# A mixture-of-experts stage: the float32 tile at place 1, gating in three steps 1024 wide, transposes evicted three tiles later

## The chip, the cores and the metric

One core of a Trainium2 chip runs the whole program. The time is that of the device for one execution, in microseconds (us), as the median of several runs; a profile is one more execution with its own time.

## The reference

Three transformer blocks follow each other on 256 tokens of width 1024. The change touches only the last part of the third, a mixture of 32 experts with 4 chosen for each token:

```python
N_EXPERTS = 32; TOP_K = 4; D_FF_EXPERT = 1024
SWIGLU_ALPHA = 1.702; SWIGLU_LIMIT = 7.0

def clamped_swiglu(u):
    u_glu, u_lin = u[..., ::2], u[..., 1::2]
    u_glu = jnp.minimum(u_glu, SWIGLU_LIMIT)
    u_lin = jnp.clip(u_lin, -SWIGLU_LIMIT, SWIGLU_LIMIT)
    return u_glu * jax.nn.sigmoid(SWIGLU_ALPHA * u_glu) * (u_lin + 1.0)

def moe_ffn(h, router_w, router_b, w1, b1, w2, b2):
    ...
    gate = jax.nn.softmax(top_val, axis=-1)
    ...
    def block_ffn(args):
        xb, e = args
        act = clamped_swiglu(xb @ w1[e] + b1[e])
        return act @ w2[e] + b2[e]
    ...
    return jnp.zeros((T, D), h.dtype).at[sorted_tok].add(contrib)
```

## The kernel before

In the mixture the experts are sorted by their number of tokens and taken one a round, `r` = 0 to 31. A round streams twelve weight tiles of 128x2048 float32 (1 MB each) from memory: eight for the first product (`up`, here u0 to u7) and four for the second (`down`, here d0 to d3). `down` in round `r` belongs to an expert of an earlier round, `r - 2` from round 6 on.

**Where a tile lives.** The SP queue issues every load in program order. Five buffers (`raw`) and a sixth (`rawm`) are used in turn, so the load of a tile waits until the tile six places ahead of it has been released.

**What is done with a tile.** Most tiles are split (`split`, L509 and L510): ACT writes a rounded copy `whi`, then DVE subtracts it and writes the rest `wlo`. TensorE multiplies the gathered tokens with both. Three pairs of `whi`, `wlo` exist; a pair comes free when TensorE has done with its `wlo`. A split tile releases its `raw` buffer when DVE has read it. To unload ACT and DVE, two tiles of a round are not split (`parts` returns `True`): TensorE reads them as plain float32 from `raw`, in eight matmuls, and releases the buffer itself. One is in `up`, one is d1 in `down`. This holds for rounds 4 to 31 ("small" experts, up to 64 tokens); rounds 0 to 3 ("big", up to 128 tokens, `r < BIGS`) have no plain tile and three matmul terms for each tile.

**Gating.** Two small experts share one tile `ml` of 128 partitions, 64 each. `take` brings the product of a round from PSUM into `ml`: ACT copies the gate and up values across the partitions (L1894), DVE adds the other half (L1895). In each even round from 6 to 30 the pair before is gated (`activate`): a minimum (L1874) and a two-sided bound (L1876) on DVE, Silu on ACT (L1875), and the product on DVE (L1880). TensorE then transposes the result (`turn`, tile `atp`, L1911), and ACT and DVE evict it into the split pair `tp` (L1921, L1922), which `down` reads. `weigh` (L1937, L1938) evicts the product of `down` as `yh`, `yl`; `combine` (L1948) multiplies it back to the tokens, and DVE adds that to `acc` (L1956).

**What sets the order.** The order on TensorE, ACT and DVE is that of the code. `at(r, slot, f)` puts a step at a slot of a round: slots 0 to 7 are the tiles of `up`, 8 to 11 those of `down`. In slot k the split of tile k comes first, then its `whi` matmuls, then the steps of the slot, then its `wlo` matmuls. `pair_of(step, r, slot)` runs `step` at `slot` and what it returns (the eviction) two slots later.

An even round with `activate` is called an even stage below, the round after it an odd one; together they stream 24 tiles.

Of the kernel before, what the change touches and what calls it, by code (L numbers as in the profile page):

```python
# [13 lines left out]
F32R = mybir.dt.float32r  # L14
# [10 lines left out]
ALPHA = 1.702  # L25
# [409 lines left out]
class Net:  # L435
# [1202 lines left out]
    def moe(s, x, nm, ctx):  # L1638
# [163 lines left out]
        def parts(what, r, k):  # L1802
# [4 lines left out]
            if not big(r) and k == (3 if what == "up" else 1):  # L1807
                return True, (w,)
# [69 lines left out]
        def gated(b, n):  # L1878
            ns, us = slice(n * 512, n * 512 + 512), slice(1024 + n * 512, 1536 + n * 512)
            nc.vector.scalar_tensor_tensor(b[:, us], b[:, us], 1.0, b[:, ns], op0=ALU.add, op1=ALU.mult)  # L1880

        def take(r, n):

            p = P[r]
            if n == 0 and (big(r) or r % 2 == 0):
                A[r] = mp.tile([128, 2048], F32, name="ml", tag="ml", bufs=1)
            if big(r):
                gate_(A[r], p[:, 0:1024], p[:, 1024:2048], n)
                return
            b = A[r - r % 2]  # L1890
            own = slice(64 * (r % 2), 64 * (r % 2) + 64)
            other = slice(64 - 64 * (r % 2), 128 - 64 * (r % 2))
            ns = slice(n * 1024, n * 1024 + 1024)
            nc.scalar.activation(b[own, ns], p[other, ns], AF.Copy)  # L1894
            nc.vector.tensor_add(b[own, ns], b[own, ns], p[own, ns])  # L1895

        def activate(r, n):
            b = A[r]
            if not big(r):
                gate_(b, b[:, 0:1024], b[:, 1024:2048], n)  # L1900
            gated(b, n)

        def turn(r, n):

            b = A[r]
            if n == 0:
                P["t"] = s.bank("atp", (128, 8, 128), "p2", 1), mp.tile([128, 8, 2, 128], F32R, name="tp",
                                                                       tag="tp", bufs=1)
            p, t = P["t"]
            for k in range(4 * n, 4 * n + 4):  # L1910
                nc.tensor.transpose(p[:, k], b[:, 1024 + k * 128:1152 + k * 128], ident)  # L1911
            if big(r):
                hi, lo = t[:, :, 0], t[:, :, 1]
# [337 lines left out]
```

## Time and profile before

| | |
|---|---|
| median of 3 runs | 2924.27 us (2922.13 to 2938.32) |
| profiled execution | 2929.59 us, of which the span from first to last instruction is 2927.8 us |
| mean granted TensorE clock | 0.968 of full speed |
| busy shares of the span | TensorE matmul 95%, DVE 77%, ACT 58% |
| bytes moved by DMA | 727.41 MB, mean 248 GB/s |

A busy share is over the whole program. The mixture is the last third, from about 1690 us on.

### The profile page before, as it was taken

How to read it: one execution, taken by the hardware profiler on the slowest of the kernel's cores; microseconds unless marked ns; L12 is line 12 of the kernel's file. 1: busy time of each engine (PE TensorE's matmuls, PEld its weight loads, DVE VectorE, ACT ScalarE, POOL GpSimd, SP SyncE). 2: the span in 40 equal slices, each digit the busy share in tenths (PEclk: the TensorE clock that was granted, in tenths of full speed). 3: DMA queues.
4: the chain of work that ended last, by engine and by line, in shares of the span. 5: the costliest groups of instructions: out<-in, count | busy, mean ns of one | idle time of the engine just before them, and what ended most of it. 6: DMA issues, size and time to landing. Idle time of an engine off the chain costs nothing. (4 is left out here: it accounts for less than half of the span.)

```text
span 2927.8 us, 46001 instructions
## 1 busy us (share of the span) xinstructions
PE 2778.3 (95%) x17764; PEld 2391.2 (82%) x17764; DVE 2256.4 (77%) x3587; ACT 1691.8 (58%) x2676; POOL 3.3 (0%) x10
## 2 busy tenths in 40 slices
PE   9999999999999999999999989989998999999986
PEld 9999999999989999899998677766666666666664
DVE  7676787787777778887777558788888888888885
ACT  6554454644545447644665456666666666666663
POOL 0000000000000000000000000000000000000000
PEclk9999999999999999999999989999999999999998
DMA  7655566576536664366423238788888888888884
GB/s 281 230 203 185 182 243 251 189 272 239 194 116 223 252 238 159 116 244 245 144 101 110 92 149 315 291 324 345 348 354 346 347 355 347 349 343 347 350 356 162
DMA packets 102146, 727.41 MB, mean 248 GB/s; under 512 B 11352, under 2 KB 12888, under 8 KB 14368
## 3 DMA queue, kind: packets, MB, share of 16 engines
q1 hardware_dynamic: 99648, 719.64, 64.6%
q10 hardware_dynamic: 2272, 4.75, 0.5%
q8 instruction: 143, 2.34, 0.3%
q14 instruction: 83, 0.68, 0.1%
HBM read 723.28 MB, written 1.06 MB: 247 GB/s over the span
## 5 line engine op out<-in xcount | busy, mean ns | idle before, releaser
L510 DVE TENSOR_TENSOR wlo<-raw,whi 128x512 fp32r<-128x512 f32 (+1 forms) x1267 | 1247.1, 1019 | 217.7 <-ACT whi L509 212.5
L509 ACT ACTIVATE whi<-raw 128x512 fp32r<-128x512 f32 (+1 forms) x1267 | 1065.1, 891 | 516.1 <-issue 280.1
L515 PE MATMUL gu<-xh,whi 128*128 128x256 f32 (+1 forms) x1760 | 499.7, 284 | 1.7 <-ACT whi L509 1.7
L517 PE MATMUL gu<-xh,wlo 128*128 128x256 f32 (+1 forms) x1760 | 497.5, 283 | 0.7 <-DVE wlo L510 0.7
L516 PE MATMUL gu<-xl,whi 128*128 128x256 f32 (+1 forms) x1760 | 498.0, 283 | 0.0
L1843 PE MATMUL p<-whi,gx 128*128 128x512 f32 x1040 | 300.9, 417 | 49.1 <-ACT whi L509 49.1
L517 PEld LDWEIGHTS gu<-xh,wlo 128*128 128x128 f32 x1760 | 333.8, 190 | 1.1 <-DVE wlo L510 0.9
L515 PEld LDWEIGHTS gu<-xh,whi 128*128 128x128 f32 x1760 | 332.4, 189 | 2.5 <-ACT whi L509 2.1
L516 PEld LDWEIGHTS gu<-xl,whi 128*128 128x128 f32 x1760 | 332.9, 189 | 0.3
L1843 PE MATMUL p<-wlo,gx 128*128 128x512 f32 x912 | 283.1, 435 | 40.4 <-DVE wlo L510 39.5
L1843 PEld LDWEIGHTS p<-whi,gx 128*128 128x128 f32 x1040 | 199.0, 196 | 108.7 <-ACT whi L509 64.6
L1843 PEld LDWEIGHTS p<-wlo,gx 128*128 128x128 f32 x912 | 170.7, 204 | 103.4 <-DVE wlo L510 75.7
L517 PE MATMUL acc<-fh,wlo 128*128 128x256 f32 x880 | 245.5, 280 | 0.0
L516 PE MATMUL acc<-fl,whi 128*128 128x256 f32 x880 | 244.9, 280 | 0.1
L515 PE MATMUL acc<-fh,whi 128*128 128x256 f32 x880 | 242.4, 280 | 0.0
L510 DVE TENSOR_TENSOR wlo<-rawm,whi 128x2048 fp32r<-128x2048 f32 x63 | 144.0, 2286 | 51.0 <-ACT whi L509 51.0
L516 PEld LDWEIGHTS acc<-fl,whi 128*128 128x128 f32 x880 | 165.8, 188 | 0.6 <-DVE fl L510 0.4
L517 PEld LDWEIGHTS acc<-fh,wlo 128*128 128x128 f32 x880 | 165.2, 188 | 0.0
L515 PEld LDWEIGHTS acc<-fh,whi 128*128 128x128 f32 x880 | 163.2, 187 | 1.2 <-ACT fh L509 0.8
L1865 PE MATMUL p<-whi,tp 128*128 128x512 f32 x464 | 152.2, 418 | 1.8 <-ACT whi L509 1.8
L1865 PE MATMUL p<-wlo,tp 128*128 128x512 f32 x400 | 128.7, 403 | 16.9 <-DVE wlo L510 16.9
L509 ACT ACTIVATE whi<-rawm 128x2048 fp32r<-128x2048 f32 x63 | 120.4, 1912 | 27.8 <-DMA rawm<-wmoe 26.4
(704 smaller groups left out, 4918.2 us busy)
## 6 DMA issues: line engine op xcount, KB each, us to landing
raw<-wmoe SPq DMA_DIRECT2D x321, 1024.0 KB, 7.4
raw<-wf SPq DMA_DIRECT2D x164, 1024.0 KB, 4.9
rawm<-wmoe SPq DMA_DIRECT2D x63, 1024.0 KB, 6.7
raw<-win SPq DMA_DIRECT2D x26, 1024.0 KB, 4.8
raw<-wada SPq DMA_DIRECT2D x24, 1024.0 KB, 4.8
raw<-wmod SPq DMA_DIRECT2D x24, 1024.0 KB, 4.9
raw<-wain SPq DMA_DIRECT2D x14, 1024.0 KB, 4.8
raw<-wkvf SPq DMA_DIRECT2D x9, 1024.0 KB, 4.8
```

Of the source, the lines that this page charges most:

```text
L509: a = s.nc.scalar.activation(hi, x, AF.Copy)
L510: s.nc.vector.tensor_sub(lo, x, hi.bitcast(F32))
L515: mm(out, w[0], x[0], start=first, stop=False, skip_group_check=True)
L516: mm(out, w[0], x[1], start=False, stop=False, skip_group_check=True)
L517: mm(out, w[1], x[0], start=False, stop=last, skip_group_check=True)
L1843: mm(p[:, ns], xi, wi[:, ns], start=k == 0 and j == 0, stop=False, skip_group_check=True)
L1865: mm(p[:, n * 512:n * 512 + 512], xi, wi[:, c:c + 512], start=k == 0 and j == 0, stop=k == 7 and j == len(ts) - 1, skip_group_check=True)
```

## The change

The plain tile of `up` is u1 instead of u3. `activate` becomes three steps in three slots: both bounds on DVE at slot 0 (`bound`), Silu on ACT at slot 1 (`silu`), the product on DVE at slot 2 (`gated`), each over 1024 columns in one instruction where there were two of 512. All eight transposes are issued at slot 3 (half of them stood at slot 4), and their two evictions at slots 6 and 7 instead of 5 and 6. The two ACT copies of `take` stand together at slot 10, ahead of both additions (`fold`). For the big rounds `take` only bounds, and Silu moves into the next round's slot 1. The tail after the last round is written with the new steps.

```diff
-            if not big(r) and k == (3 if what == "up" else 1):
+            if not big(r) and k == 1:
                 return True, (w,)
...
-        def gate_(b, g, u, n):
-            ns, us = slice(n * 512, n * 512 + 512), slice(1024 + n * 512, 1536 + n * 512)
-            nc.vector.tensor_scalar(b[:, ns], g[:, ns], 7.0, None, op0=ALU.min)
-            nc.scalar.activation(b[:, ns], b[:, ns], AF.Silu, scale=ALPHA)
-            nc.vector.tensor_scalar(b[:, us], u[:, ns], 7.0, -7.0, op0=ALU.min, op1=ALU.max)
...
+        def bound(b, g, u):
+            nc.vector.tensor_scalar(b[:, 0:1024], g, 7.0, None, op0=ALU.min)
+            nc.vector.tensor_scalar(b[:, 1024:2048], u, 7.0, -7.0, op0=ALU.min, op1=ALU.max)
+
+        def silu(r):
+            nc.scalar.activation(A[r][:, 0:1024], A[r][:, 0:1024], AF.Silu, scale=ALPHA)
+
+        def gated(r):
+            b = A[r]
+            nc.vector.scalar_tensor_tensor(b[:, 1024:2048], b[:, 1024:2048], 1.0, b[:, 0:1024], op0=ALU.add,
+                                           op1=ALU.mult)
...
+            own, other = halves(r)
+            for ns in (slice(0, 1024), slice(1024, 2048)):
+                nc.scalar.activation(A[r - r % 2][own, ns], p[other, ns], AF.Copy)
...
-            for k in range(4 * n, 4 * n + 4):
+            for k in range(8):
                 nc.tensor.transpose(p[:, k], b[:, 1024 + k * 128:1152 + k * 128], ident)
...
             if t >= 0:
-                for n in range(2):
-                    at(r, n, lambda t=t, n=n: activate(t, n))
-                    pair_of(lambda t=t, n=n: turn(t, n), r, 3 + n)
+                at(r, 0, lambda t=t: activate(t))
+                at(r, 1, lambda t=t: silu(t))
+                at(r, 2, lambda t=t: gated(t))
+
+                def turned(t=t, r=r):
+                    out = turn(t)
+                    at(r, 6, lambda: out(0))
+                    at(r, 7, lambda: out(1))
+                at(r, 3, turned)
             if r != 0:
-                at(r, 9 if r == BIGS else 10, lambda r=r: take(r, 0))
-                at(r, 9 if r == BIGS else 11, lambda r=r: take(r, 1))
+                at(r, 9 if r == BIGS else 10, lambda r=r: take(r))
+                at(r, 9 if r == BIGS else 10, lambda r=r: fold(r, 0))
+                at(r, 9 if r == BIGS else 11, lambda r=r: fold(r, 1))
```

ACT, from d2 of an odd round into the even round 20 behind it. Before (`whi<-raw` and `whi<-rawm` are splits, `ml<-p` a copy of `take`, `ml<-ml` a Silu, `yh` a `weigh`, `tp` an eviction of transposes):

```order
L509 ACTIVATE whi<-rawm 128x2048
L1894 ACTIVATE ml<-p_25096 64x1024
L509 ACTIVATE whi<-raw 128x2048
L1894 ACTIVATE ml<-p_25096 64x1024
L509 ACTIVATE whi<-raw 128x2048
L1875 ACTIVATE ml<-ml 128x512
L509 ACTIVATE whi<-raw 128x2048
L1937 ACTIVATE yh<-p_25285,gs 128x512
L1875 ACTIVATE ml<-ml 128x512
L509 ACTIVATE whi<-raw 128x2048
L1937 ACTIVATE yh<-p_25285,gs 128x512
```

The same place after the change:

```order
L509 ACTIVATE whi<-rawm 128x2048
L1893 ACTIVATE ml<-p_25052 64x1024 x2
L509 ACTIVATE whi<-raw 128x2048 x2
L1940 ACTIVATE yh<-p_25241,gs 128x512
L1877 ACTIVATE ml<-ml 128x1024
L509 ACTIVATE whi<-raw 128x2048
L1940 ACTIVATE yh<-p_25241,gs 128x512
L509 ACTIVATE whi<-raw 128x2048
L509 ACTIVATE whi<-rawm 128x2048
L509 ACTIVATE whi<-raw 128x2048 x2
L1929 ACTIVATE tp<-atp 128x8x64
```

Both copies now precede the split of d3, one Silu of twice the width stands ahead of the split of u2, and four splits (u3 to u6) stand between the last `yh` and the first eviction; before, two (u4 and u5) did.

DVE in the same even round, from the split of u0 (`wlo`) on. Before:

```order
L510 TENSOR_TENSOR wlo<-raw,whi 128x2048
L1874 TENSOR_SCALAR ml<-ml 128x512
L1876 TENSOR_SCALAR ml<-ml 128x512
L1880 SCALAR_TENSOR_TENSOR ml<-ml 128x512
L510 TENSOR_TENSOR wlo<-raw,whi 128x2048
L1938 SCALAR_TENSOR_TENSOR yl<-p_25285,gs,yh 128x512
L1874 TENSOR_SCALAR ml<-ml 128x512
L1876 TENSOR_SCALAR ml<-ml 128x512
L1880 SCALAR_TENSOR_TENSOR ml<-ml 128x512
L510 TENSOR_TENSOR wlo<-raw,whi 128x2048
```

After:

```order
L510 TENSOR_TENSOR wlo<-raw,whi 128x2048
L1873 TENSOR_SCALAR ml<-ml 128x1024
L1874 TENSOR_SCALAR ml<-ml 128x1024
L1941 SCALAR_TENSOR_TENSOR yl<-p_25241,gs,yh 128x512
L510 TENSOR_TENSOR wlo<-raw,whi 128x2048
L1941 SCALAR_TENSOR_TENSOR yl<-p_25241,gs,yh 128x512
L1881 SCALAR_TENSOR_TENSOR ml<-ml 128x1024
L510 TENSOR_TENSOR wlo<-raw,whi 128x2048
L510 TENSOR_TENSOR wlo<-rawm,whi 128x2048
L510 TENSOR_TENSOR wlo<-raw,whi 128x2048
```

The bounds follow the split of u0 in both, but the product now stands behind the split of u2, and no split of u1 is left between them.

TensorE at the start of `up` in the same even round (`p<-raw` is the plain tile, eight matmuls that are printed as x4 by their operands; `atp` the transposes). Before:

```order
L1843 MATMUL p_25342<-whi,gx 128x512 x4
L1843 MATMUL p_25342<-wlo,gx 128x512 x4
L1843 MATMUL p_25342<-raw,gx 128x512 x4
L1911 MATMUL atp<-const,ml 128x128 x4
L1843 MATMUL p_25342<-whi,gx 128x512 x4
```

After:

```order
L1843 MATMUL p_25298<-wlo,gx 128x512 x4
L1843 MATMUL p_25298<-raw,gx 128x512 x4
L1843 MATMUL p_25298<-whi,gx 128x512 x4
L1843 MATMUL p_25298<-wlo,gx 128x512 x4
L1843 MATMUL p_25298<-whi,gx 128x512 x4
L1918 MATMUL atp<-const,ml 128x128 x8
L1843 MATMUL p_25298<-wlo,gx 128x512 x4
```

The plain tile, which stood right ahead of the transposes, now stands behind the first split tile, and the transposes stand inside the fourth tile.

## Rows read from the trace of the kernel before

**Rows 1.** The page's second part: GB/s in the 40 equal slices of the span (73.2 us each).

```profile
GB/s 281 230 203 185 182 243 251 189 272 239 194 116 223 252 238 159 116 244 245 144 101 110 92 149 315 291 324 345 348 354 346 347 355 347 349 343 347 350 356 162
```

**Rows 2.** Windows: the stretch; its length; busy time of PE, PEld, DVE, ACT and POOL with instructions; granted clock; DMA share; GB/s. The second row holds the rounds from the first even stage to the last, the others pieces of one pair of rounds.

```profile
2476.00:2514.00 38.00, 32.50 (x120) 21.54 (x118) 32.38 (x20) 25.07 (x17) 0.00 (x0) 1.00 1.01 423
...
1930.00:2870.00 940.00, 852.43 (x3404) 598.60 (x3404) 775.34 (x596) 626.59 (x536) 0.00 (x0) 0.93 0.87 347
...
2442.50:2453.00 10.50, 8.53 (x16) 4.90 (x17) 8.99 (x9) 6.61 (x5) 0.00 (x0) 0.51 0.81 321
```

**Rows 3.** Timeline of ACT: start, duration, line, operation, [idle before, and what ended it]. The first Silu of the even stages of rounds 8 and 30.

```profile
2003.10 0.63 ACT L1875 ACTIVATE ml<-ml 128x512 f32<-128x512 f32 x1 [3.28 <-DVE ml L1874]
...
2799.77 0.63 ACT L1875 ACTIVATE ml<-ml 128x512 f32<-128x512 f32 x1 [3.28 <-DVE ml L1874]
```

**Rows 4.** What waited for what from 1930 to 2870 us: total us, times, longest. (SPq is the queue that issues the loads.)

```profile
DVE wlo L510 <- ACT whi L509: 87.3, 93, 4.6
...
ACT tp L1921 <- PE atp L1911: 98.9, 13, 8.4
ACT ml L1875 <- DVE ml L1874: 82.7, 27, 3.3
...
SPq L490 <- PE p L1865: 133.2, 26, 5.6
SPq L490 <- PE p L1843: 132.9, 26, 6.9
```

**Rows 5.** Timeline of ACT in one pair of rounds, from d2 of the odd round ahead (2426.13) to the next such d2 (2497.65).

```profile
2426.13 1.92 ACT L509 ACTIVATE whi<-rawm 128x2048 fp32r<-128x2048 f32 x1 [0.65 <-DMA rawm<-wmoe]
2428.07 1.02 ACT L1894 ACTIVATE ml<-p 64x1024 f32<-64x1024 f32 x1
...
2437.90 0.63 ACT L1875 ACTIVATE ml<-ml 128x512 f32<-128x512 f32 x1 [3.28 <-DVE ml L1874]
...
2458.00 0.60 ACT L1921 ACTIVATE tp<-atp 128x512 fp32r<-128x512 f32 x1 [7.59 <-PE atp L1911]
...
2482.73 1.91 ACT L509 ACTIVATE whi<-rawm 128x2048 fp32r<-128x2048 f32 x1 [0.76 <-DMA rawm<-wmoe]
2485.22 1.92 ACT L509 ACTIVATE whi<-raw 128x2048 fp32r<-128x2048 f32 x1 [0.58 <-DMA raw<-wmoe]
...
2497.65 1.91 ACT L509 ACTIVATE whi<-rawm 128x2048 fp32r<-128x2048 f32 x1 [3.06 <-DMA rawm<-wmoe]
```

**Rows 6.** Timeline of DVE in the same even stage.

```profile
2430.40 1.22 DVE L1895 TENSOR_TENSOR ml<-ml,p 64x1024 f32<-64x1024 f32 x1
...
2437.44 0.42 DVE L1874 TENSOR_SCALAR ml<-ml 128x512 f32<-128x512 f32 x1
2437.78 0.42 DVE L1876 TENSOR_SCALAR ml<-ml 128x512 f32<-128x512 f32 x1
2438.56 0.69 DVE L1880 SCALAR_TENSOR_TENSOR ml<-ml 128x512 f32<-128x512 f32 x1 [0.36 <-ACT ml L1875]
2440.36 2.29 DVE L510 TENSOR_TENSOR wlo<-raw,whi 128x2048 fp32r<-128x2048 f32 x1 [1.10 <-ACT whi L509]
2442.69 0.75 DVE L1938 SCALAR_TENSOR_TENSOR yl<-p,gs,yh 128x512 fp32r<-128x512 f32 x1
...
2458.63 0.69 DVE L1922 SCALAR_TENSOR_TENSOR tp<-atp,tp 128x512 fp32r<-128x512 f32 x1 [5.01 <-ACT tp L1921]
...
2463.84 2.28 DVE L510 TENSOR_TENSOR wlo<-raw,whi 128x2048 fp32r<-128x2048 f32 x1
2466.05 0.68 DVE L1956 TENSOR_TENSOR acc<-acc,cbp 128x512 f32<-128x512 f32 x1
2466.65 2.28 DVE L510 TENSOR_TENSOR wlo<-raw,whi 128x2048 fp32r<-128x2048 f32 x1
```

**Rows 7.** Timeline of TensorE in the same even stage: the split tiles u0 to u2, the plain u3, the second group of transposes and what follows it, the `whi` terms of two successive tiles with a combine between them (2458.74, 2461.53), and d0 and the plain d1.

```profile
2435.79 1.08 PE L1843 MATMUL p<-whi,gx 128*128 128x512 f32 x4
2437.58 1.20 PE L1843 MATMUL p<-wlo,gx 128*128 128x512 f32 x4 [0.71 <-DVE wlo L510]
2440.38 1.20 PE L1843 MATMUL p<-whi,gx 128*128 128x512 f32 x4 [1.60 <-ACT whi L509]
2442.71 2.07 PE L1843 MATMUL p<-wlo,gx 128*128 128x512 f32 x4 [1.13 <-DVE wlo L510]
2446.29 2.07 PE L1843 MATMUL p<-whi,gx 128*128 128x512 f32 x4 [1.51 <-ACT whi L509]
...
2450.49 4.73 PE L1843 MATMUL p<-raw,gx 128*128 128x512 f32 x8
...
2457.37 0.60 PE L1911 MATMUL atp<-const,ml 128*128 128x128 f32 x4
...
2458.74 1.07 PE L1843 MATMUL p<-whi,gx 128*128 128x512 f32 x4
...
2461.53 1.08 PE L1843 MATMUL p<-whi,gx 128*128 128x512 f32 x4
...
2468.98 0.74 PE L1865 MATMUL p<-wlo,tp 128*128 128x512 f32 x2 [0.20 <-DVE wlo L510]
...
2470.48 3.60 PE L1865 MATMUL p<-raw,tp 128*128 128x512 f32 x8
2473.52 1.03 PE L1865 MATMUL p<-whi,tp 128*128 128x512 f32 x2
```

More of the change, by code (lines that the diff above doesn't have):

```diff
@@ L1884, in take @@
+        def take(r):
             p = P[r]
-            if n == 0 and (big(r) or r % 2 == 0):
+            if big(r) or r % 2 == 0:
                 A[r] = mp.tile([128, 2048], F32, name="ml", tag="ml", bufs=1)
             if big(r):
-                gate_(A[r], p[:, 0:1024], p[:, 1024:2048], n)
+                return bound(A[r], p[:, 0:1024], p[:, 1024:2048])
+            own, other = halves(r)
+            for ns in (slice(0, 1024), slice(1024, 2048)):
+                nc.scalar.activation(A[r - r % 2][own, ns], p[other, ns], AF.Copy)
@@ L1889, in take, with halves, fold @@
+        def halves(r):
+            h = 64 * (r % 2)
+            return slice(h, h + 64), slice(64 - h, 128 - h)
+        def fold(r, n):
+            if big(r):
                 return
-            b = A[r - r % 2]
-            own = slice(64 * (r % 2), 64 * (r % 2) + 64)
-            other = slice(64 - 64 * (r % 2), 128 - 64 * (r % 2))
+            own, _ = halves(r)
             ns = slice(n * 1024, n * 1024 + 1024)
-            nc.scalar.activation(b[own, ns], p[other, ns], AF.Copy)
-            nc.vector.tensor_add(b[own, ns], b[own, ns], p[own, ns])
@@ L1897, in activate @@
-        def activate(r, n):
-            b = A[r]
[L1899 to L1909, printed above, removed]
-            for k in range(4 * n, 4 * n + 4):
+            b = A[r - r % 2][own, ns]
@@ L1911, in turn, with activate @@
+            nc.vector.tensor_add(b, b, P[r][own, ns])
+        def activate(r):
+            if not big(r):
+                bound(A[r], A[r][:, 0:1024], A[r][:, 1024:2048])
+        def turn(r):
+            b = A[r]
+            p = s.bank("atp", (128, 8, 128), "p2", 1)
+            t = mp.tile([128, 8, 2, 128], F32R, name="tp", tag="tp", bufs=1)
+            for k in range(8):
                 nc.tensor.transpose(p[:, k], b[:, 1024 + k * 128:1152 + k * 128], ident)
             if big(r):
-                hi, lo = t[:, :, 0], t[:, :, 1]
+                hi, lo = A[r] = t[:, :, 0], t[:, :, 1]
@@ L2024, in moe @@
                         bias2(c2)
-                    take(0, 0)
-                    take(0, 1)
+                    take(0)
                     for k in range(8, 12):
@@ L2044, in moe @@
                     run(r, 11)
-            for n in range(2):
-                activate(30, n)
+            activate(30)
+            silu(30)
             weigh(29, 0)
             weigh(29, 1)
-            outs = [turn(30, n) for n in range(2)]
+            gated(30)
+            out = turn(30)
             for c2 in range(4):
@@ L2052, in moe @@
                 if c2 % 2:
-                    outs[c2 // 2]()
+                    out(c2 // 2)
             for _ in down(30, 32):
```

12 lines of the change are left out of this document (2 added, 10 removed).

## The prediction

> **What bounds the kernel now.** I first looked at the bytes by slices, because the mixture streams its weights: the last sixteen slices sit between 315 and 356 GB/s with little variation, which looks like a limit [rows 1]. It is not one. Cut finer, the mean of 347 GB/s over the rounds with even stages hides 38 us at 423 GB/s, with the DMA engines busy all the time, and poorer stretches between [rows 2]. In the good stretch tiles land 2.49 us apart (2482.73 and 2485.22, both splits having waited for the transfer) [rows 5]. A pair of rounds streams 24 tiles, so it needs 24 x 2.49 = 59.8 us. It takes more: from the first Silu of round 8 to that of round 30 there are eleven pairs in 796.7 us, 72.4 us each [rows 3]. The pair shown, from one d2 to the next, takes 2497.65 - 2426.13 = 71.5 us [rows 5], 11.7 above its transfers. The mixture is held up by something that recurs in every pair.
>
> The list of waits names it: ACT waits for the transposes 13 times, 98.9 us in all, and for DVE's bound before a Silu, 82.7 us; the load queue waits for TensorE, which alone releases plain tiles, 266 us [rows 4]. The three timelines of one even stage show the order of events. Gating alternates between DVE and ACT twice, and each time a split of ACT is queued behind a Silu: DVE stands idle 0.36 us, then 1.10 [rows 6], and again so in the second half. TensorE starves in these gaps (0.71, 1.60, 1.13 and 1.51 us) [rows 7], and the granted clock over the next 10.5 us is 0.51, the lower of its two levels, 1.2 GHz [rows 2]. There it comes to the plain u3, which takes 2450.49 to about 2455.05, and only behind that do the transposes stand; the second group ends at 2457.97 [rows 7]. ACT's eviction was queued ahead of the split of u6, so ACT idles 7.59 us [rows 5] and DVE 5.01 [rows 6]. Meanwhile every buffer is full, and the transfers stop. So what decides is the chain of DVE and ACT through an even stage, and then the plain d1, whose release lets the queue go on.
>
> **The change, by replaying this stage with the new order.** I keep the start (d2 on ACT at 2426.13) and use the durations of these rows.
>
> *Take.* Both copies precede the split of d3 on ACT: 2428.07 + 2 x 1.02 = 2430.1, d3 until 2432.05. DVE has finished its addition at 2431.62 [rows 5, 6], so its split of d3 waits 0.43 us; from there to the end of u0's split everything is 0.43 later than the 2437.44 at which it now goes on: 2437.9. The copies themselves are the same four a pair.
>
> *Bounds.* 512 columns follow each other on DVE at 0.34 us, so 1024 take at most 0.68 each, 1.36 for both: until 2439.3. A lower bound for both is 0.84 (two at the present 0.42). I take 1.36, since no row shows the wider form. The `yl` behind them ends near 2440.0 (0.75).
>
> *Silu, the new wait.* 0.63 us for 512 columns and 1.91 for the 2048 of a split give 0.43 us for each further 512, so 1.06 for 1024; twice 0.63 is the upper bound [rows 5]. Silu runs from 2439.3 to 2440.4, and the split of u2, queued behind it on ACT, until 2442.3. DVE waits for that split from 2440.0: 2.3 us. TensorE has the plain u1 then (0.38 us a matmul at the full clock, 3.04 for eight, by 2470.48 to 2473.52 [rows 7]): it starts behind u0's `wlo` (from 2437.9, 1.0 us) and ends near 2442, so it hides the stall from TensorE.
>
> *Product, then a run without waits on DVE.* u2 ends at 2444.6; the second `yl` takes 0.7, the product 1.22 (0.69 at 512, 2.29 for a subtraction of 2048, 0.53 per 512 between them [rows 6]): 2446.5. Back to back, a split occupies DVE 2.21 us and an addition to `acc` or an eviction 0.60 (2463.84, 2466.05, 2466.65 [rows 6]). u3, u4 and u5 end at 2453.1; then come an addition, u6, an eviction and an addition, u7, the same two again, and d0: 3 x 2.21 + 5 x 0.60 = 9.6, so d0 ends at 2462.7. Now it ends about 2468.9 (the 2.28 that begins at 2466.65). That is 6.2 us.
>
> *Do the others keep up?* At the full clock TensorE needs 2.8 us for a split tile with its combine (2458.74 to 2461.53, without a wait [rows 7]), DVE 2.2 + 0.6 to 1.2 for the same tile: TensorE stays within about 1 us of DVE. The transposes wait for the product until 2446.5 and take at most 1.2 (four in 0.60); behind them TensorE's `wlo` of u3 waits for DVE until 2448.7 anyway. Their evictions come about 4 us later in the queue, when the transposes are long done: the 7.59 and 5.01 us vanish, and until `down` needs `tp` at 2462 there is room. If that room were gone, each us would come back on the start of d0.
>
> *Out of the stage.* The plain d1 starts 1.5 us after DVE ends d0 now (2470.48), so at 2464.2, and ends at 2467.3 instead of 2473.5. From the latter to the landing of the next d2 there were 24.1 us [rows 5, 7], in which transfers set the pace; I keep them. The pair becomes 41.1 + 24.1 = 65.2 us, **6.3 us less**. They hold seven tiles (17.4 us at 2.49) and 6.7 us in which the queue gets going again; d2, d3 and u0 are released 6.2 us earlier too, and if 2 of these 6.7 us are saved with them, the pair loses 8.3, my bound upwards. In the odd stage the plain tile at place 1 is released later than a split one, but it also stands right behind the stage whose stall already holds the queue, so I cost it at nothing; if its cover fails, one tile's 2.49 us a pair is lost.
>
> *The rest.* Even stages are those of rounds 6 to 30, 13 of them, as 13 waits for transposes show [rows 4]: 13 x 6.3 = 82 us. Six of them also build a gather; that work is in both orders. In the big rounds three terms of four matmuls a tile, at about 1.0 us each (1.07 at 2458.74 [rows 7]), exceed DVE's 2.3 us a tile, so moved gating lies under matmuls: nothing. In the tail the product comes behind both `yl` and before the transposes, up to 1.3 us lost. Sum: 2929.6 - 82 + 1 = 2849 us for the profiled execution. That execution lies 5 us (0.2%) above the median of the runs, 2924.3; a median for the changed kernel would be about 2845.
>
> **Two rules weighed.** Rows give 423 GB/s for 38 us on end [rows 2], so a pair can go down to 59.8 us. The Trainium skill, "SBUF — State Buffer", Summary: rules for kernel authors, tells one to estimate transfers from HBM at about 358 GB/s. By that a pair (25.2 MB) needs 70.3 us and the change could save only some 1.2 us a pair, 16 in all; the trace disagrees.
>
> **The rivals.**
> *The clock falls again (0.2).* In the replay TensorE still waits, 1.15 us before u0's `wlo`, 0.3, 1.35 before u2's and 1.2 before u3's: 4.0 us in 13, against 5.0 now. If that again brings the lower level, for 7 to 9 us instead of 10.5, TensorE does 3.5 to 4.5 us less work and has 1 us of slack, so d1 comes about 3 us late: 3.3 us a pair saved, 43 in all, 2886 (the median). For it: the waits are shorter, not gone. Against: the plain tile fills the longest. The Trainium skill, "TensorE: Matmul & The Clock Gate", HAM oscillation, likewise has groups of matmuls with waits between them throttled anew; the 0.51 in the rows agrees.
> *The transfers hold it anyway (0.1).* The gain of the even stage returns because the queue, which is in order, stops at another plain tile. For it: 266 us of the queue's waits are for TensorE. Then 0 to 2 us a pair: 2898 to 2924, in the middle 2911.
> *Slower (0.08).* The low clock spreads over the whole even stage, because Silu, product and transposes now stand one behind the other across three tiles and each gap feeds the next. Half the clock for X us takes X/2 of TensorE's work; 1 us of slack and the 6.3 saved are used up at X = 14.6. At 20 us a pair loses 2.7, 35 in all: 2959. Against it: the plain tile, 3 us of work with no split before it.
> *More is gained (0.07):* the queue restarts at once, and the bounds take their lower price: 8.8 us a pair, 114: 2811.
>
> **How the numbers follow.** My forecast (0.55) is the replay, 2845, with 2822 (8.3 a pair less tail) to 2870 (4 a pair) as its own range. A run can tell about 0.5%, 14.6 us, from no change. The forecast, the gain beyond it, and the clock rival lie below 2909; so does part of the transfer rival: faster 0.84, same 0.08, slower 0.08. From 2811 to 2904 the range leaves out the slower case, most of the transfer rival and a little below.
>
> **What will show it.** Right: ACT's wait for transposes gone from the list; the first Silu of successive even stages 65 us apart; DVE without waits from the product to d0; one wait of about 2.3 us for the split of u2; a granted clock near 1 through the stage; above 380 GB/s over the rounds. Wrong: a low clock in the same place, a wait of DVE on ACT for pairs of `whi` not yet released, or a load queue whose waits for TensorE have moved to the other plain tile.

## The result

The changed kernel takes **2820.52 us** (median of 4 runs, 2813.82 to 2830.34) against 2931.30 us for the kernel before (4 runs, 2922.13 to 2939.76): a ratio of **0.9625**, 95% interval 0.9575 to 0.9676. The forecast was 2845 us, its range 2811 to 2904. The profiled execution took 2826.35 us, its span 2824.6 us; all stretches of the changed kernel below are of that execution.

### The profile page after: what moved, and what is told of

It is laid out like the page before. It is cut to its first block, busy times and chain, and to the rows that moved or that the text cites. A ratio compares the mean times of both kernels' runs of the same rounds, so it can differ in the third digit from the quotient of the medians.

```text
span 2824.6 us, 45877 instructions
## 1 busy us (share of the span) xinstructions
PE 2732.6 (97%) x17764; PEld 2371.8 (84%) x17764; DVE 2245.6 (80%) x3533; ACT 1687.9 (60%) x2658; POOL 3.3 (0%) x10
## 5 line engine op out<-in xcount | busy, mean ns | idle before, releaser
L1843 PE MATMUL p<-whi,gx 128*128 128x512 f32 x1040 | 290.1, 405 | 2.5 <-ACT whi L509 2.5
L1843 PE MATMUL p<-wlo,gx 128*128 128x512 f32 x912 | 260.3, 407 | 31.1 <-DVE wlo L510 29.2
L1843 PEld LDWEIGHTS p<-wlo,gx 128*128 128x128 f32 x912 | 158.4, 189 | 86.5 <-DVE wlo L510 62.5
L1865 PE MATMUL p<-wlo,tp 128*128 128x512 f32 x400 | 128.3, 402 | 18.6 <-DVE wlo L510 18.6
```

Source lines behind the costliest of these rows:

```text
L1843: mm(p[:, ns], xi, wi[:, ns], start=k == 0 and j == 0, stop=False, skip_group_check=True)
L1865: mm(p[:, n * 512:n * 512 + 512], xi, wi[:, c:c + 512], start=k == 0 and j == 0, stop=k == 7 and j == len(ts) - 1, skip_group_check=True)
```

## The profile after

Two lines of the page's second part, the granted clock (a 9 is 90% or more) and the GB/s in 40 slices of 70.6 us:

```profile
PEclk9999999999999999999999988999999999999998
...
GB/s 290 226 222 165 182 227 247 240 208 245 204 182 162 225 245 209 135 198 251 199 100 126 115 72 136 352 311 386 396 387 399 376 396 384 390 373 388 390 398 165
```

Where the page before showed 343 to 356 [rows 1], the mixture's slices now show 373 to 399. Windows, with the columns of [rows 2]: from the first Silu of round 8's stage to that of round 30's, and the 10.5 us behind the Silu of one stage (that of round 20, which is also the one shown below).

```profile
1992.25:2706.55 714.30, 678.35 (x2882) 486.12 (x2881) 648.67 (x468) 527.35 (x442) 0.00 (x0) 1.00 0.97 389
2382.00:2392.50 10.50, 9.26 (x36) 5.87 (x35) 8.93 (x7) 9.97 (x7) 0.00 (x0) 1.00 1.01 407
```

The granted clock of the rounds went from 0.93 to 1.00. Where 10.5 us of the stage had 0.51 before [rows 2], the 10.5 us behind Silu have 1.00, the upper of the two levels, 2.4 GHz, and the DMA engines do not pause in them (407 GB/s). The two Silus that bound the first window (timeline of ACT, as [rows 3]):

```profile
1992.25 1.06 ACT L1877 ACTIVATE ml<-ml 128x1024 f32<-128x1024 f32 x1 [1.04 <-DVE ml L1873]
...
2706.55 1.06 ACT L1877 ACTIVATE ml<-ml 128x1024 f32<-128x1024 f32 x1 [1.78 <-DVE ml L1873]
```

Eleven pairs in 714.3 us are **64.94 us a pair**, where it was 72.42. The list of waits from 1930 to 2760 us, to be held against [rows 4]:

```profile
ACT yh L1940 <- PE p L1865: 63.7, 25, 3.9
ACT tp L1929 <- DVE tp L1930: 44.8, 13, 3.6
...
ACT ml L1877 <- DVE ml L1873: 18.6, 12, 1.8
...
DVE wlo L510 <- ACT whi L509: 70.7, 60, 3.3
...
SPq L490 <- PE p L1865: 125.9, 25, 5.6
SPq L490 <- PE p L1843: 112.1, 26, 4.9
```

ACT no longer waits for the transposes; the largest wait of an engine in the list before (98.9 us) is gone. ACT's wait for a bound fell from 82.7 to 18.6 us. Its longest wait is now that of `yh` for the product of `down`, 63.7 us; in the even stage shown it ends before the bound that Silu waits for, and so costs nothing there. That the second eviction on ACT now waits for DVE's first one (44.8 us) costs nothing, since DVE works without a break there. The load queue's waits for TensorE, 238 us, are still there and only a little shorter. The prediction named these alone, but most of the queue's waiting was and is for DVE to finish a split and so release its buffer:

```profile
SPq L490 <- DVE wlo L510: 414.8, 147, 5.8
```

```profile
SPq L490 <- DVE wlo L510: 335.9, 166, 3.4
```

The first line is of the kernel before (1930 to 2870 us), the second of the changed one (1930 to 2760).

Three timelines of the stage, in the columns of [rows 5], [rows 6] and [rows 7]. ACT, from d2 of the odd round ahead to the next such d2:

```profile
2369.65 1.92 ACT L509 ACTIVATE whi<-rawm 128x2048 fp32r<-128x2048 f32 x1
2371.59 1.93 ACT L1893 ACTIVATE ml<-p 64x1024 f32<-64x1024 f32 x2
...
2382.00 1.06 ACT L1877 ACTIVATE ml<-ml 128x1024 f32<-128x1024 f32 x1 [1.15 <-DVE ml L1873]
2382.96 1.89 ACT L509 ACTIVATE whi<-raw 128x2048 fp32r<-128x2048 f32 x1
...
2393.19 0.58 ACT L1929 ACTIVATE tp<-atp 128x512 fp32r<-128x512 f32 x1
...
2399.01 0.60 ACT L1929 ACTIVATE tp<-atp 128x512 fp32r<-128x512 f32 x1 [3.24 <-DVE tp L1930]
...
2433.87 1.91 ACT L509 ACTIVATE whi<-rawm 128x2048 fp32r<-128x2048 f32 x1 [3.06 <-DMA rawm<-wmoe]
```

DVE, from the split of u0 to the split of d0:

```profile
2379.07 2.29 DVE L510 TENSOR_TENSOR wlo<-raw,whi 128x2048 fp32r<-128x2048 f32 x1
2381.28 0.69 DVE L1873 TENSOR_SCALAR ml<-ml 128x1024 f32<-128x1024 f32 x1
2381.88 0.69 DVE L1874 TENSOR_SCALAR ml<-ml 128x1024 f32<-128x1024 f32 x1
2382.60 0.75 DVE L1941 SCALAR_TENSOR_TENSOR yl<-p,gs,yh 128x512 fp32r<-128x512 f32 x1
2384.89 2.29 DVE L510 TENSOR_TENSOR wlo<-raw,whi 128x2048 fp32r<-128x2048 f32 x1 [1.54 <-ACT whi L509]
2387.10 0.74 DVE L1941 SCALAR_TENSOR_TENSOR yl<-p,gs,yh 128x512 fp32r<-128x512 f32 x1
2387.76 1.21 DVE L1881 SCALAR_TENSOR_TENSOR ml<-ml 128x1024 f32<-128x1024 f32 x1
2388.89 2.28 DVE L510 TENSOR_TENSOR wlo<-raw,whi 128x2048 fp32r<-128x2048 f32 x1
...
2402.89 2.28 DVE L510 TENSOR_TENSOR wlo<-raw,whi 128x2048 fp32r<-128x2048 f32 x1
```

TensorE: u0, the plain u1, the later terms of u2 and u3 (the others stand between them without a wait), and the plain d1:

```profile
2381.42 1.21 PE L1843 MATMUL p<-wlo,gx 128*128 128x512 f32 x4 [0.38 <-DVE wlo L510]
2382.46 3.60 PE L1843 MATMUL p<-raw,gx 128*128 128x512 f32 x8
...
2387.24 1.21 PE L1843 MATMUL p<-wlo,gx 128*128 128x512 f32 x4 [0.25 <-DVE wlo L510]
...
2391.23 1.21 PE L1843 MATMUL p<-wlo,gx 128*128 128x512 f32 x4 [0.99 <-DVE wlo L510]
...
2406.72 3.60 PE L1865 MATMUL p<-raw,tp 128*128 128x512 f32 x8
```

DVE has one wait between u0 and d0, 1.54 us, and it lies beside the plain u1 (2382.46 to about 2385.5). TensorE waits 0.38, 0.25 and 0.99 us where it waited 0.71, 1.60, 1.13 and 1.51 [rows 7]. The evictions come when the transposes have long been done.

## A measure for the experiments: DVE's idle time in the even part

The start of the plain d1 in the odd stage to that of the plain d1 in the even stage behind it is called the even part here. In round 20 it is 41.78 us before and 33.85 us after. One window each, of that round, with the columns of [rows 2]; the third busy time is DVE's. Before:

```profile
2428.70:2470.48 41.78, 36.38 (x141) 25.07 (x140) 33.15 (x27) 25.29 (x20) 0.00 (x0) 0.88 0.84 335
```

After:

```profile
2372.87:2406.72 33.85, 32.03 (x141) 23.26 (x140) 31.84 (x24) 24.56 (x19) 0.00 (x0) 1.00 1.01 409
```

DVE was idle for 41.78 - 33.15 = 8.63 us and is idle for 33.85 - 31.84 = 2.01 us, and its busy time shrank by 1.31 us. Of that, 0.66 us goes with three 1024-wide steps in place of six 512-wide ones; the other 0.65 is only where the window cuts the split of d2, of which it holds 1.67 us before and 1.02 after. 6.62 + 1.31 make up the 7.93 us of the even part's gain. TensorE's busy time in the window fell too, from 36.38 to 32.03 us, because its matmuls there ran at the full clock: the two engines are now about equally full. Round 20 is one of the shorter stages; every second one is some 2.5 us longer in both kernels. Over the twelve even parts of rounds 8 to 30 the mean falls from 42.8 to 35.4 us, while the odd part between them, from one plain d1 to the next, is 29.6 us on the mean in both kernels. So the whole gain of a pair lies in the even part. Each experiment is read by its pair and, where it helps, by this window.

| kernel | median us | ratio to before (95%) | us a pair, rounds 8 to 30 | granted clock there |
|---|---|---|---|---|
| before | 2931.30 | 1 | 72.42 | 0.93 |
| after | 2820.52 | 0.9625 (0.9575 to 0.9676) | 64.94 | 1.00 |
| u_plain3 | 2822.62 | 0.9628 (0.9577 to 0.9679) | 65.55 | 1.00 |
| u_evict56 | 2822.32 | 0.9643 (0.9588 to 0.9697) | 64.84 | 1.00 |
| u_gate512 | 2827.64 | 0.9661 (0.9605 to 0.9717) | 65.62 | 1.00 |
| o_plain1 | 2845.38 | 0.9731 (0.9700 to 0.9761) | 65.90 | 1.00 |
| o_evict3 | 2916.16 | 0.9974 (0.9957 to 0.9992) | 71.64 | 0.93 |
| o_gate3 | 2844.84 | 0.9717 (0.9693 to 0.9741) | 65.78 | 1.00 |
| c_warm | 2904.68 | 0.9932 (0.9904 to 0.9959) | 69.99 | 1.00 |
| c_warm_ev | 2891.02 | 0.9881 (0.9847 to 0.9915) | 69.39 | 1.00 |
| o_big | 2913.92 | 0.9961 (0.9934 to 0.9987) | 71.54 | 0.94 |
| v_down0 | 2817.86 | 0.9617 (0.9564 to 0.9669) | 64.89 | 1.00 |
| v_silu2 | 2812.40 | 0.9605 (0.9576 to 0.9634) | 64.15 | 1.00 |
| v_both | 2803.70 | 0.9593 (0.9552 to 0.9634) | 64.09 | 1.00 |

Each ratio is to runs of the kernel before on the same chip, which had medians of 2924 to 2931 us. The pairs come from one profiled execution each. How far they can be trusted is seen in o_big, which leaves the pairs as they were before and shows 71.54 us: differences under some 0.9 us say little by themselves. The three runs of one part alone (o_plain1, o_gate3, o_evict3) keep the big rounds as they were, which by o_big below are worth 12 us, so they are compared with the changed kernel by their pairs and not by their medians.

## Experiments: one part undone

**u_plain3**, the changed kernel with up's plain tile at its old place:

```
-            if not big(r) and k == 1:
+            if not big(r) and k == (3 if what == "up" else 1):
```

> The changed kernel with the plain tile of up back at place 3; gating in three steps and late evictions stay. Two theories. A, the order of the queues: what counts is the chain of DVE and ACT through an even stage; the split of u1 stands between the bounds and Silu, so DVE waits no more than now, and the pair stays near 65 us: 2815 to 2835 us. B, the cover of TensorE: without the plain tile under the gating, TensorE waits some 2.5 us each for the wlo of u1 and u2, the clock falls to its lower level, u3 takes over 4 us, and a pair loses 3 to 4 us: 2860 to 2875 us with a granted clock near 0.5 for some 10 us of each even stage.

Measured: 65.55 us a pair at a granted clock of 1.00. Theory A holds: the plain tile at place 3 does not by itself bring the low clock back. With gating in three steps its old place costs some 0.6 us a pair, which is within what one profile can tell.

**u_evict56**, the changed kernel with the evictions one tile earlier:

```
-                    at(r, 6, lambda: out(0))
-                    at(r, 7, lambda: out(1))
+                    at(r, 5, lambda: out(0))
+                    at(r, 6, lambda: out(1))
```

> The changed kernel with the evictions of the transposes at slots 5 and 6, as before, instead of 6 and 7. If the evictions' later place is what removed the 7.6 us wait of ACT, that wait comes back in part and a pair loses 2 to 3 us: 2845 to 2860 us. If the plain tile's move alone freed the transposes (they end about the time at which ACT has split u5), nothing is lost: 2815 to 2828 us.

Measured: 64.84 us a pair, no change, as the second theory has it. With the transposes done in time, the place of their evictions has room.

**u_gate512**, the changed kernel with the small rounds' gating in two halves again:

```
...
-                at(r, 0, lambda t=t: activate(t))
-                at(r, 1, lambda t=t: silu(t))
-                at(r, 2, lambda t=t: gated(t))
+                if big(t):
+                    at(r, 1, lambda t=t: silu(t))
+                    at(r, 2, lambda t=t: gated(t))
+                else:
+                    at(r, 0, lambda t=t: halved(t, 0))
+                    at(r, 1, lambda t=t: halved(t, 1))
...
```

`halved` does for 512 columns the minimum, Silu, the two-sided bound and the product, in that order.

> The changed kernel with the small experts' gating in two halves of 512 columns at slots 0 and 1, each half with its four instructions, as before. If the four handoffs between DVE and ACT cost what their idle rows say (2.9 us a pair), 2855 us. If only the difference in when the split of u2 begins counts, DVE starts u2 some 1.6 us later but has the product done by then (1.1 us): 0.5 us a pair lost, 2822 to 2832 us.

Measured: 65.62 us a pair, clock 1.00. ACT waits for bounds again, 56.9 us from 2000 to 2690 (15.8 in the changed kernel), yet only 0.7 us a pair are lost, no more than one profile can tell. The second theory holds. No single part, undone, takes back more than about a tenth of the gain.

## Experiments: one part alone

**o_plain1**, the kernel before with the plain tile at place 1:

```
-            if not big(r) and k == (3 if what == "up" else 1):
+            if not big(r) and k == 1:
```

> The kernel before with one edit: the plain tile of up at place 1. Theory A (queues): the gating's handoffs stay, the second group of transposes stands behind the whi of u4 and ACT's eviction, still ahead of u6, waits some 4 us for it instead of 7.6: 5 to 6 us a pair gained of the 7.5, 2840 to 2860 us. Theory B (cover of TensorE): nearly the whole gain, 2820 to 2835 us. If the three parts add up evenly, a third: 2895 us.

Measured: 65.90 us a pair, clock 1.00. The even part of round 20:

```profile
2383.31:2418.44 35.13, 32.36 (x142) 23.24 (x141) 32.72 (x27) 25.05 (x20) 0.00 (x0) 1.00 0.96 382
```

DVE's work is nearly what it was (32.72 us), its idle time 2.41 us. The median lies where theory A had it. ACT waits 2.8 us for the transposes in this stage (the theory had some 4), and that wait no longer reaches DVE.

**o_gate3**, the kernel before with the small rounds' gating in three steps:

```
...
+                if big(t):
+                    for n in range(2):
+                        at(r, n, lambda t=t, n=n: activate(t, n))
+                else:
+                    at(r, 0, lambda t=t: bound(A[t]))
+                    at(r, 1, lambda t=t: silu(A[t]))
+                    at(r, 2, lambda t=t: product(A[t]))
                 for n in range(2):
-                    at(r, n, lambda t=t, n=n: activate(t, n))
```

> The kernel before with one edit: the small experts' gating in three steps 1024 wide at slots 0, 1 and 2 (transposes and evictions as before, plain tile at place 3). Theory A: DVE's four short idle times go (2.9 us a pair), and the transposes come as much earlier, 3 to 4.5 us a pair: 2872 to 2892 us. Theory B: TensorE still starves for the wlo of u1 and u2 and the clock falls: 2900 to 2920 us.

Measured: 65.78 us a pair, clock 1.00. Its even part:

```profile
2400.90:2435.32 34.42, 32.08 (x141) 23.19 (x140) 31.84 (x24) 24.93 (x18) 0.00 (x0) 1.00 0.96 385
```

DVE is idle for 2.58 us, with the plain tile at place 3. In the same stage ACT still waits 4.3 us for the transposes, of which 1.9 reach DVE (the timeline of ACT, then DVE's list of waits from 2386 to 2456):

```profile
2422.85 0.60 ACT L1932 ACTIVATE tp<-atp 128x512 fp32r<-128x512 f32 x1 [4.26 <-PE atp L1922]
```

```profile
DVE tp L1933 <- ACT tp L1932: 1.9, 1, 1.9
```

Neither theory had this: the median of 2844.84 lies 27 us below the better of the two ranges. Theory A summed the handoffs and the earlier transposes and gave the clock no price; by c_warm below, that price of 1.6 to 2.4 us a pair makes up much of the difference.

**o_evict3**, the kernel before with the transposes evicted three tiles behind:

```
-                    pair_of(lambda t=t, n=n: turn(t, n), r, 3 + n)
+                    pair_of(lambda t=t, n=n: turn(t, n), r, 3 + n, 3)
```

> The kernel before with one edit: the evictions three slots behind their transposes (6 and 7) instead of two. Theory A: one more split of ACT and DVE runs ahead of the wait, 2 to 3 us a pair, 2890 to 2905 us. Theory B: the clock falls in the same place as before and the gain is small, 2910 to 2930 us.

Measured: 71.64 us a pair, clock 0.93, as good as nothing, as theory B has it. ACT's wait was only handed on. DVE's list of waits from 1930 to 2860 us:

```profile
DVE acc L1956 <- PE cbp L1948: 50.3, 13, 4.7
```

DVE does one split more, and then waits 13 times for the first combine, whose matmuls stand behind the same plain tile as the transposes. TensorE is late, so it matters little which of its products is asked for first.

Either of two parts alone brings about 6.6 of the 7.5 us, and each of the others adds little to it. That fits one common cause, and the clock, 0.93 in all kernels near 72 us and 1.00 in all near 65, is a candidate for it; so is DVE's idle time.

## Experiments: the clock by itself

**c_warm**, the kernel before with matmuls that nobody reads where TensorE waits; it computes the same:

```
+        def warm(r, i):
+            m = (4, 11, 9, 18, 9)
+            if r > BIGS + 1 and r % 2 == 0 and i < len(m):
+                p = aux("warm", (128, 256))
+                for _ in range(m[i]):
+                    mm(p, hh[:, 0, 0:128], hl[:, 0, 0:256], start=True, stop=True, skip_group_check=True)
...
                     if j == 0:
                         run(r, k)
+                    warm(r, 2 * k + j)
```

> The kernel before, with idle work for TensorE: in the first three tiles of every even small round 4, 11, 9, 18 and 9 matmuls of 128x256 (about 0.12 us each at the full clock) into a spare bank that nobody reads, placed where TensorE waited for the splits. No handoff of gating, no plain tile and no transpose moves. It asks whether the low clock is the cause or a part. Theory of the chain: at the full clock the last terms of u2 and the plain tile end about 1.9 us sooner, so evictions and the rest come 1.9 us sooner: the pair goes from 72.4 to about 70.5 us, the median to about 2900 us, and ACT still waits some 6 us for the transposes in each even stage. Theory of the clock: the low clock is what both successful parts (plain tile, three steps) do away with, and the rest follows from it: the granted clock goes to 1.00, the pair to 66 to 67 us and the median to 2845 to 2855 us. If the granted clock stays at 0.93, the run says nothing for either.

Measured: the granted clock is 1.00 and the pair 69.99 us, as the theory of the chain expects. The added matmuls hardly hold up the real ones: in round 20 the `wlo` term of u0 starts 2.6 us behind the start of its split, where it was 2.35, and those of u1 and u2 as before. The window over the eleven pairs, and the plain u3 of round 20, 4.73 us long before [rows 7]:

```profile
2002.95:2772.79 769.84, 747.58 (x3442) 559.74 (x3441) 656.23 (x501) 530.83 (x452) 0.00 (x0) 1.00 0.90 360
```

```profile
2435.19 3.59 PE L1850 MATMUL p<-raw,gx 128*128 128x512 f32 x8
```

DVE's list of waits in its even part (2414.87 to 2454.01, 39.14 us) shows what the clock leaves:

```profile
DVE wlo L510 <- ACT whi L509: 3.8, 4, 1.1
DVE tp L1930 <- ACT tp L1929: 3.0, 1, 3.0
DVE ml L1888 <- ACT ml L1883: 0.7, 2, 0.4
```

The handoffs of gating are there as before: 0.7 us in the last line and, of the first, two waits of 1.11 behind Silu, 2.9 in all (of its other two, one follows the eviction and one ended before the window began). The wait for the eviction fell from 5.01 us [rows 6] to 3.0. So the low clock is worth 2.4 us of the 7.5 (1.6 if o_big's 71.54 is taken for the pair before; the medians on that chip, 2926.95 and 2904.68, give 1.7 over thirteen pairs), about a third at most. The rest is order: the 3.0 behind the plain tile and the 2.9 of the handoffs.

**c_warm_ev**, the same with the eviction three tiles behind (both edits above):

> The kernel before with the same idle work for TensorE as in the run ahead (granted clock 1.00, 70.0 us a pair), and the transposes evicted three tiles behind, which alone gave nothing. It asks whether late eviction was worthless because of the low clock. If so, DVE's wait for the eviction (3.0 us in an even stage at the full clock) goes altogether: 66.5 to 67.5 us a pair and a median of 2860 to 2875 us. The other theory: as long as the plain tile stands at place 3, ahead of the transposes and of the matmuls of the first combine, DVE has only one more split that it can do before it waits for TensorE; it then waits some 2 us for the first combine in place of 3.0 for the eviction: 68.5 to 69.5 us a pair, 2885 to 2900 us.

Measured: 69.39 us a pair, 0.6 less than c_warm; by the medians it is about 1 us. In DVE's timeline of round 20 the wait for the eviction gave way to one for the first combine:

```profile
2436.66 0.69 DVE L1964 TENSOR_TENSOR acc<-acc,cbp 128x512 f32<-128x512 f32 x1 [1.98 <-PE cbp L1956]
```

That speaks for the second theory: late eviction was worth little not because of the clock but because of the plain tile, 3.6 us of TensorE's time right ahead of everything that DVE needs next. The median, 2891, lies inside the interval that this theory gave; the other asked for 2875 or less.

## Experiment: the big rounds

Between the first up matmul of the experts and the first Silu of round 6's stage, the changed kernel needs 214.3 us (1712.38 to 1926.63) and the kernel before 231.8 (1698.72 to 1930.51). The prediction had put this stretch at nothing. In the kernel before, ACT at the end of round 1, a big round:

```profile
1774.83 0.63 ACT L1875 ACTIVATE ml<-ml 128x512 f32<-128x512 f32 x1 [2.96 <-DVE ml L1874]
...
1780.23 0.63 ACT L1875 ACTIVATE ml<-ml 128x512 f32<-128x512 f32 x1 [2.96 <-DVE ml L1874]
```

DVE there, and TensorE at the first tile of the round behind it:

```profile
1777.31 2.29 DVE L510 TENSOR_TENSOR wlo<-raw,whi 128x2048 fp32r<-128x2048 f32 x1 [1.91 <-ACT whi L509]
...
1782.70 2.29 DVE L510 TENSOR_TENSOR wlo<-rawm,whi 128x2048 fp32r<-128x2048 f32 x1 [1.90 <-ACT whi L509]
```

```profile
1782.72 1.19 PE L1843 MATMUL p<-whi,gx 128*128 128x512 f32 x4 [0.47 <-ACT whi L509]
...
1785.05 1.20 PE L1843 MATMUL p<-wlo,gx 128*128 128x512 f32 x4 [1.13 <-DVE wlo L510]
```

Each Silu holds the splits queued behind it on ACT for 2.96 us, and DVE stands still 1.9 us for each. **o_big** is the kernel before with the big rounds' gating alone in three steps:

```
             if big(r):
-                gate_(A[r], p[:, 0:1024], p[:, 1024:2048], n)
+                if n == 0:
+                    nc.vector.tensor_scalar(A[r][:, 0:1024], p[:, 0:1024], 7.0, None, op0=ALU.min)
+                    nc.vector.tensor_scalar(A[r][:, 1024:2048], p[:, 1024:2048], 7.0, -7.0, op0=ALU.min,
+                                            op1=ALU.max)
                 return
...
+                if big(t):
+                    at(r, 1, lambda t=t: silu(A[t]))
+                    at(r, 2, lambda t=t: product(A[t]))
                 for n in range(2):
-                    at(r, n, lambda t=t, n=n: activate(t, n))
+                    if not big(t):
+                        at(r, n, lambda t=t, n=n: activate(t, n))
```

> The kernel before, with the gating of the big rounds 0 to 3 alone in three steps (both bounds 1024 wide at once at slot 10, Silu at slot 1 of the next round, product at slot 2); the small rounds stay as they were. The prediction put this at nothing, because TensorE's matmuls were to cover it: then about 2924 us, and the time from the first up matmul of the experts to the first small round's copy out of PSUM stays at 197 us. The other theory: before, ACT waits 2.96 us for a bound six times in these rounds with splits queued behind it, and DVE then waits 1.9 us each time for these splits, more than TensorE's slack of about 0.4 us a tile can cover; then that time falls by 12 to 16 us to 182 to 185, the pairs of small rounds stay at 72.4 us, and the median is 2908 to 2913 us.

Measured: from the first up matmul to the first copy of a small round 185.35 us, where it was 197.63 (182.75 in the changed kernel); 2913.92 us, a ratio of 0.9961 (0.9934 to 0.9987). The theory of the waits was right: 12.3 us in the big rounds, at the lower end of what it gave. One profile of each could mislead, but the same stretch takes 193.8 to 198.8 us in the six profiled kernels with the old gating of the big rounds and 181.0 to 185.4 in the eight with the new. The changed kernel has 2.6 more in the same stretch, and 2.7 between that copy and the Silu of round 6; neither was taken apart further.

## Experiments: what binds now

**v_down0**, the changed kernel with down's plain tile at place 0:

```
-            if not big(r) and k == 1:
+            if not big(r) and k == (1 if what == "up" else 0):
```

> The changed kernel with the plain tile of down at place 0 instead of 1 (rounds from 4 on). If the load queue's stop of some 4 us behind the plain d1 of an even stage is what keeps a pair at 65 us above the 59.8 of its transfers, an earlier release (TensorE needs no split for d0 and starts it as soon as the bias is done, some 2.3 us earlier) takes 2 us off a pair: 2790 to 2800 us. If DVE's work sets the pair, nothing: 2815 to 2825 us.

Measured: 64.89 us a pair, no change. The gain of 2 us a pair did not come. ACT's waits for tiles in `raw` rose from 13.6 to 33.7 us between 2000 and 2690 (those for `rawm` fell from 14.7 to 5.9), which fits a queue that got no further ahead.

**v_silu2**, the changed kernel with Silu behind the split of u2 in the small rounds, product and transposes one tile later:

```
-                at(r, 1, lambda t=t: silu(t))
-                at(r, 2, lambda t=t: gated(t))
+                at(r, 1 if big(t) else 2, lambda t=t: silu(t))
+                at(r, 2 if big(t) else 3, lambda t=t: gated(t))
...
-                at(r, 3, turned)
+                at(r, 3 if big(t) else 4, turned)
```

> The changed kernel with Silu at slot 2, behind the split of u2, the product at slot 3 and the transposes at slot 4 in the small rounds. DVE's wait of 1.5 us for the split of u2 goes. If DVE's chain sets the even stage, 1.5 us a pair, 2797 to 2807 us; if the load queue or TensorE does, nothing: 2815 to 2825 us.

Measured: 64.15 us a pair, 0.8 less than the changed kernel. DVE's wait of 1.54 us is gone, but one of 0.64 comes in ahead of the next split (the second `yh` now stands ahead of Silu on ACT and waits for DVE). The even part of round 20:

```profile
2365.27:2398.10 32.83, 31.72 (x142) 23.26 (x141) 31.73 (x24) 24.86 (x19) 0.00 (x0) 1.00 0.99 403
```

DVE's idle time in it fell from 2.01 to 1.10 us. The median of 2812.40 lies between the two ranges expected: DVE's chain still counts, but only half of its wait came back.

**v_both**, the two edits together:

> The changed kernel, with Silu of the small rounds moved behind the split of u2 (product and transposes one tile later) and down's plain tile at place 0. The chain: Silu at slot 2 alone gave 0.8 us a pair, down's plain tile at 0 alone nothing; with DVE's wait gone the queue may now be what sets the pair, and an earlier plain d0 lets it go on some 2 us sooner: 62.5 to 63.5 us a pair, 2790 to 2805 us. If the transfers behind the plain tile of down are not what sets the pair, both together give what Silu alone gives: 64.1 us, 2810 to 2816 us.

Measured: 64.09 us a pair, what Silu alone gave. Of the two theories the second holds for the pair. The median of 2803.70 is nevertheless the lowest of all and lies in the range of the first. Of the 14.2 us by which its profiled span is shorter than that of v_silu2, 8.9 lie ahead of the experts, where the two programs are the same. The interval of its ratio (0.9552 to 0.9634) overlaps those of v_silu2 and the changed kernel, so that a version faster than the latter is likely (two kernels with Silu moved show 64.1 us a pair) but not shown.

## Why the prediction was right, and where its sizes were off

**The chain of DVE and ACT in the even stage decides: right.** The replay, shifted so that both stages begin at their d2, beside the trace (predicted, then measured, in us behind d2):

| step | predicted | measured |
|---|---|---|
| bounds begin | 11.8 | 11.6 |
| Silu begins | 13.2 | 12.35 |
| split of u2 begins on DVE | 16.2 | 15.2 |
| product ends, DVE goes on | 20.4 | 19.2 |
| d0 split ends | 36.6 | 35.4 |
| plain d1 begins | 38.1 | 37.1 |
| next d2 | 65.2 | 64.2 |

**The one term of the replay that was mis-sized is the new wait for Silu.** It was put behind both bounds, at 2.3 us of idle time for DVE. In the trace Silu is released by the first bound alone (L1873) and starts while DVE does the second; with bounds 0.60 us apart instead of 0.68, DVE's wait is 1.54 us. That is 0.8 of the 1.0 us by which the measured pair of round 20 is shorter, and it goes unchanged down to d1. The 24.1 us behind the plain d1, which the prediction kept, are 24.1 again (from about 2409.76 to 2433.87), and the odd stage, put at nothing, cost nothing: 29.6 us in both.

**The sum.** The span of the profiled executions shrank by 103.2 us, which divides as follows:

| stretch | predicted gain | measured gain |
|---|---|---|
| up to the experts' first up matmul (1698.72, 1712.38) | 0 | -13.7 |
| from there to the first Silu of round 6's stage | 0 | 17.5 |
| thirteen pairs, to the Silu of the tail (2868.43, 2768.24) | 82 | 96.3 |
| the tail | -1.3 | 3.0 |

Thirteen pairs gained 7.4 us each instead of 6.3, on the mean of all pairs. Some of the prediction's medians are about 4 us off by its own terms: its own range should read 2818 to 2874 instead of 2822 to 2870, and the clock rival 2883 instead of 2886. The measured 2820.5 is at the lower end of that range. The part ahead of the experts is the same program in both, and its end varies from 1698.7 to 1714.2 us among the profiled executions of the kernels here; it is no effect of the change, and what makes it vary stays open.

**The step that failed is the one on the big rounds**, "moved gating lies under matmuls: nothing". It compared DVE's busy time per tile with TensorE's and left out ACT: two waits of 2.96 us a round in ACT's queue, with splits behind them, are more than TensorE's slack can take up, some half a us a tile (three terms that follow each other at 0.91 us against a split of 2.2). They stood in the trace of before, six of them in that stretch, which the prediction did not look at, since it read ACT's list only from 1930 us on. What it put at nothing is 12.3 us by o_big and 17.5 in the sum above. The error was of the same sign as the other, and so the forecast came out 24 us too high. That the wider range still held was in part luck: its lower end was set for a queue that restarts at once, which did not happen, and the big rounds took up that room.

**The tail.** The product stands behind both `yl`, as forecast, but TensorE's transposes start no later for it: they waited 5.5 us for the second `yl` before, and 5.4 for the product after. The granted clock over the tail is 0.82 where it was 0.77, and TensorE is busy for 32.8 us in it instead of 37.0; that goes with the 3.0 us, but why the clock is higher there stays open.

**The rivals.** *The clock falls again* did not happen; TensorE's waits were 1.6 us in that stretch, not the 4.0 of the replay. The price that the rival gave the clock, some 3 us a pair, was somewhat high: c_warm measures 1.6 to 2.4. The Trainium skill, "TensorE: Matmul & The Clock Gate", HAM oscillation, has groups of matmuls with waits for DMA between them throttled anew; c_warm, which only fills TensorE's waits for the splits, agrees, and those 1.6 to 2.4 us are what the fall costs here. *The transfers hold it anyway* fell: the pair shortened by all that the even part gave back. By the rule of the Trainium skill in "SBUF — State Buffer", Summary: rules for kernel authors, about 358 GB/s, the estimate for a pair is 70.3 us; eleven pairs at 389 GB/s disagree. *Slower* fell with the clock rival. *More is gained* was half right: the bounds held Silu up by less than forecast, but the queue did not restart sooner.

**Of the signs named beforehand** all came but the size of one: no wait of ACT for transposes, Silus 65 us apart, DVE without waits from the product to d0, a clock of 1.00, 389 GB/s; the wait for u2 is there, at 1.54 us instead of 2.3.

**What no reading of one trace could tell** is that the parts are not additive. The replay moved all of them together. Alone, the plain tile gives 6.5 us a pair and the three steps 6.6, the late eviction 0.8 at most, and the whole change 7.5. The two copies of `take` side by side and the eight transposes in one slot were not run alone. In the even part DVE has 8.6 us of idle time in two kinds, the handoffs and the lateness of TensorE. The plain tile at place 1 gives TensorE work during a handoff and takes the plain tile away from ahead of the transposes; the three steps take one handoff away, and with it the low clock and most of the lateness. Either one leaves 2.4 to 2.6 us of idle time, and below that lie DVE's work, about 31.8 us, and TensorE's, about 32, which the other part cannot remove. That these are near the floor now is read from the windows, and v_silu2, with 1.10 us of idle time left, gained only 0.8 more; no kernel with less work for either was run.

## What to carry over

Where one engine's idle time has two causes in the same stretch, fixing either may take nearly all of it, so cost a change of several parts down to a floor (the busy time of the fullest engine) and not as a sum of parts. A wait on an engine that is not the bottleneck counts for what is queued behind it: read the list of waits for every stretch that the change touches, also for those where the bottleneck seems to have slack. Moving the reader of a late product only hands the wait to the next reader, as late eviction did here; what has to move is the work that makes the producer late.

## What the hardware showed beyond that

The bounds of 1024 columns in SBUF follow each other on DVE at 0.60 us, against 0.34 for 512, and the product of 1024 takes 1.21 us: two halves cost only 0.08 us more than one wide bound, so the gain of 1024 lies mostly in the handoff saved and not in the instructions. The granted clock stayed at 1.00 with waits of 0.38, 0.25 and 0.99 us left, and matmuls that compute nothing, some 6 us of them in each even stage, made a kernel faster by 0.7% (0.9932, 0.9904 to 0.9959).
